# Gate and up projections of a feed-forward layer by seven half products, with weight sums on GpSimd

## The chip, the cores and the metric

The kernel runs on one core of a Trainium2 chip. The metric is the device time of one execution in microseconds. The engines are TensorE (PE for its matmuls, PEld for its weight loads), VectorE (DVE), ScalarE (ACT), GpSimd (POOL) and SyncE (SP, which issues the large loads). Each runs its instructions in a fixed order and waits on semaphores for the others.

## The reference

Two transformer blocks over 512 tokens of width 1024. The end of the second block is the part that changes:

```python
D_FF = -(-8 * D_MODEL // (3 * 256)) * 256          # 2816
...
def swiglu(h, w_gate, w_up, w_down):
    return (jax.nn.silu(h @ w_gate) * (h @ w_up)) @ w_down
...
h2 = modulate(rms_norm_2(x, g_pre_ffn[l]), sh_f, sc_f)
x = x + gt_f * rms_norm_2(swiglu(h2, w_gate[l], w_up[l], w_down[l]), g_post_ffn[l])
```

`h` is 512 x 1024, the gate and up weights are 1024 x 2816, the down weights 2816 x 1024, all float32.

## The kernel before

Every float32 operand of these products is split into a high part rounded to fp32r and the rest (`hi`, `lo`), and each product is three matmuls: hi·hi, hi·lo and lo·hi (`mm3`, lines 235 to 237). The normed tokens lie in SBUF with the 1024 input features on partitions, as eight slices `k` of 128, in two pairs of tiles `hi0`, `lo0` (slices 0 to 3) and `hi1`, `lo1` (slices 4 to 7), each 128 x 4 x 512. In the page and the trace all of these read `hi` and `lo`, and buffers' numbers are left out.

The weights come in chunks of 512 columns (`chunk`, line 210: one load of 2 MB into one of three buffers). For each slice k of a chunk, `split` makes `whi` on ScalarE (line 228, a copy that rounds) and `wlo` on VectorE (line 229, the chunk less `whi`, both in SBUF). There are three buffers of each, so that the splits can run up to three slices ahead of TensorE. TensorE then does 12 matmuls of 512 tokens for that slice (four groups of 128 columns, three matmuls each).

`phase3` ends with `mix_out`, `gate_first` and `ffn`. `gate_first` does the gate's first 512 columns in two halves of 256 tokens, since the last tokens' norms are still being made; in its second half each slice is split again, for 12 matmuls of 256 tokens. In `ffn` the order is up 0, gate 1, up 1, and so on to gate 5 and up 5 (the sixth chunk has 256 columns). After a gate chunk ScalarE applies silu from PSUM into `act` (line 1790), after an up chunk VectorE multiplies from PSUM (line 1792). Then comes the down projection.

The order on each engine comes from the scheduler of the tile framework; it puts instructions of a later step early where it can, but an engine that has reached an instruction waits for what that instruction needs, with all behind it.

Of the kernel before, what the change touches and what calls it, by code (L numbers as in the profile page):

```python
# [20 lines left out]
P = 128  # L21
# [94 lines left out]
class K:  # L116
# [101 lines left out]
    def split(self, src, gain=None, dst=None, eng=None):  # L218

        nc = self.nc  # L220
        m, n = src.shape
        if dst is None:
            dst = [self.sp.tile([P, 512], F32R, tag=f"w{b}", name=self.name(f"w{b}"))[:m, :n] for b in ("hi", "lo")]
        if gain is not None:
            self.split_to(*dst, src, gain)
            return dst
        hi, lo = dst
        nc.scalar.activation(hi, src, AF.Copy)  # L228
        (eng or nc.vector).tensor_tensor(lo, src, hi.bitcast(F32), ALU.subtract)  # L229
        return hi, lo  # L230
# [1080 lines left out]
    def phase3(self, u, banks):  # L1311
        tc = self.tc
        pool = lambda nm: tc.tile_pool(name=nm, bufs=1, reuse_waits="tile")
        with contextlib.ExitStack() as again:
            with pool("mix") as self.pm:

                self.mix = [None, None]
                heads = pool("heads")
                self.ph = heads.__enter__()
                with pool("p3f") as p:  # L1320
                    self.fourier(p, u)
                banks.close()
                with pool("p3b") as p:
                    self.attend2(p)
                heads.__exit__(None, None, None)
                again.enter_context(self.banks())
                with pool("p3c") as p:
                    y = p.tile([P, NT, D], F32, name="y_mix")
                    ready = self.mix_out(p, y)
                    halves = [self.half(0), self.half(1)]  # L1330
# [414 lines left out]
    def gate_first(self, hx, tiles, ready):  # L1745
# [16 lines left out]
                    self.mm3(ac[j][:, c], (wh[:, s], wl[:, s]), hx(k, c), k == 0, k == KD - 1)  # L1762
        return ac

    def ffn(self, p, hx, first):
# [4 lines left out]
        gm = self.post_gain(p, 1)  # L1770
        act = T([P, NF, S], "act")
        wg, wu = (I[n][0].rearrange("(k p) n -> p k n", p=P) for n in ("w_gate_2", "w_up_2"))
        for c in range(6):
            f = 4 if c < 5 else 2
            cs = slice(c * 512, c * 512 + f * P)
            for m, src in enumerate((wg, wu)):
                if c + m:
                    w = self.chunk(src[:, :, cs])
                    ac = self.others() if m else [self.accum() for _ in range(f)]
                    for k in range(KD):  # L1780
                        wh, wl = self.split(w[:, k, :])
                        for j in range(f):
# [4 lines left out]
                for j in range(f):  # L1787
                    a = act[:, 4 * c + j, :]
                    if m == 0:
                        sc.activation(a, ac[j], AF.Silu)  # L1790
                    else:
                        v.tensor_tensor(a, ac[j], a, ALU.mult)
        wd = I["w_down_2"][0].rearrange("(j p) n -> p j n", p=P)
        y = T([P, NT, D], "y")
        ss = self.sm.tile([P, NT, 2], F32, tag="ssy", name=self.name("ssy"))
        junk = lambda: T([P, S], "h", bufs=2)
        for n in range(2):
            cs = slice(n * 512, n * 512 + 512)
            ac = [self.accum() for _ in range(NT)]
            for c in range(3):  # L1800
                nj = 8 if c < 2 else 6
                w = self.chunk(wd[:, c * 8:c * 8 + nj, cs])
                last = n == 1 and c == 2
                if last:
                    wb = self.split_big(w)
                ab = []
                for i in range(nj):
                    j = 8 * c + i
                    if i % 4 == 0:
                        hb = self.half(j // 4 % 2)  # L1810
# [36 lines left out]
```

## Time and profile before

| | |
|---|---|
| three runs | 1512.69, 1518.17 and 1518.07 us (median 1518.07) |
| the profiled execution | 1516.21 us, its span 1514.4 us |
| mean granted TensorE clock | 0.971 |
| PE busy over the span | 1432.1 us, 95% |
| DVE, ACT, POOL busy | 720.6 us, 502.1 us, 123.8 us |
| second half of the gate's first chunk to the end of up 5 | about 1147 us to 1382.6 us of the span |
| down projection and tail | 1382.6 us to the end |

The page names a group of instructions by line, engine and operation with its tiles; the trace gives for each its start, its duration, and what the engine waited for before it. A row of the timeline with x3 is three instructions in a row, and its duration is that of all three.

### The profile page before, as it was taken

What the parts mean: (1) busy time and instruction counts of PE and PEld (TensorE: products, weight loads), DVE (VectorE), ACT (ScalarE), POOL (GpSimd) and SP (SyncE); (2) the same over time, 40 slices, a digit from 0 to 9 for tenths busy, and PEclk for the clock granted to TensorE, in tenths of its full rate; (3) what the DMA queues carried; (4) which work ended last, traced back from release to release, by engine and by line L of the source; (5) the groups of instructions that cost most, each with busy time, mean ns of one, the idle gap of its engine ahead of it and who ended that gap; (6) DMA issues with size and microseconds to landing.
All of it is one profiled execution on the core that took longest, in us unless ns stands there. A gap on an engine that the chain in (4) does not pass through costs nothing. (4 is left out here: it accounts for less than half of the span.)

```text
span 1514.4 us, 20068 instructions
## 1 busy us (share of the span) xinstructions
PE 1432.1 (95%) x7322; PEld 962.0 (64%) x7322; DVE 720.6 (48%) x1907; ACT 502.1 (33%) x1031; POOL 123.8 (8%) x145
## 2 busy tenths in 40 slices
PE   8999999998988999999999698999989999999997
PEld 6776657587434434433433387888878888888886
DVE  5465487867224322321222486667575333325356
ACT  5344454644101000100000454556445222224351
POOL 0012122301000000000000230110011000000000
PEclk9999997996999999999999899999999999999999
DMA  7647761061999999999999601110032331223211
GB/s 249 204 154 216 248 219 56 1 256 78 343 405 420 413 409 421 415 409 418 418 409 416 250 33 41 57 56 2 16 137 99 111 112 57 83 84 109 101 42 56
DMA packets 91957, 303.81 MB, mean 201 GB/s; under 512 B 6432, under 2 KB 12208, under 8 KB 79440
## 3 DMA queue, kind: packets, MB, share of 16 engines
q1 hardware_dynamic: 90016, 299.02, 51.4%
q0 software_dynamic: 1712, 3.35, 0.8%
q8 instruction: 59, 0.97, 0.3%
q14 instruction: 42, 0.34, 0.1%
q10 hardware_dynamic: 128, 0.13, 0.0%
HBM read 297.82 MB, written 2.56 MB: 198 GB/s over the span
## 5 line engine op out<-in xcount | busy, mean ns | idle before, releaser
L1268 PE MATMUL acc<-w,xg 128*32 128x512 f32 (+1 forms) x1024 | 216.1, 601 | 3.9 <-DMA w<-in_w_dram 3.9
L229 DVE TENSOR_TENSOR wlo<-w,whi 128x512 fp32r<-128x512 f32 (+3 forms) x161 | 104.0, 648 | 207.7 <-ACT whi L228 190.3
L228 ACT ACTIVATE whi<-w 128x512 fp32r<-128x512 f32 (+2 forms) x177 | 104.7, 596 | 219.0 <-PE o L236 86.2
L1268 PEld LDWEIGHTS acc<-w,xg 128*32 128x32 f32 (+1 forms) x1024 | 56.9, 124 | 122.8 <-issue 98.4
L1290 PE MATMUL acc<-w,hid 128*32 128x512 f32 (+1 forms) x512 | 120.8, 607 | 0.8 <-ACT hid L1281 0.7
L235 PE MATMUL acc<-whi,hi 128*128 128x512 f32 x280 | 112.4, 404 | 0.4 <-ACT hid L726 0.4
L236 PE MATMUL acc<-wlo,hi 128*128 128x512 f32 x280 | 112.3, 401 | 0.0
L237 PE MATMUL acc<-whi,lo 128*128 128x512 f32 x280 | 111.4, 398 | 0.0
L235 PE MATMUL acc<-hi,whi 128*128 128x512 f32 (+1 forms) x272 | 100.2, 372 | 2.8 <-ACT hi L1702 2.4
L237 PE MATMUL acc<-hi,wlo 128*128 128x512 f32 (+1 forms) x272 | 100.9, 372 | 0.6 <-POOL wlo L229 0.6
L236 PE MATMUL acc<-lo,whi 128*128 128x512 f32 (+1 forms) x272 | 101.0, 372 | 0.3 <-DVE lo L1703 0.2
L1275 DVE SCALAR_TENSOR_TENSOR hid<-acc,gc,hid 128x512 f32<-128x512 f32 x12 | 9.0, 751 | 158.1 <-PE acc L1268 142.6
L1290 PEld LDWEIGHTS acc<-w,hid 128*32 128x32 f32 (+1 forms) x512 | 37.8, 125 | 72.7 <-issue 59.3
L1305 DVE TENSOR_TENSOR x_sb<-ps,x_sb 128x512 f32<-128x512 f32 x96 | 60.6, 684 | 22.9 <-PE ps L1304 22.7
L235 PE MATMUL ps<-hi,whi 128*128 128x512 f32 x160 | 64.0, 400 | 0.0
L237 PE MATMUL ps<-hi,wlo 128*128 128x512 f32 x160 | 63.5, 397 | 0.0
L236 PE MATMUL ps<-lo,whi 128*128 128x512 f32 x160 | 63.5, 397 | 0.0
L235 PEld LDWEIGHTS acc<-whi,hi 128*128 128x128 f32 x280 | 52.9, 190 | 15.3 <-issue 1.4
L236 PEld LDWEIGHTS acc<-wlo,hi 128*128 128x128 f32 x280 | 53.0, 189 | 13.6 <-issue 1.8
L237 PEld LDWEIGHTS acc<-whi,lo 128*128 128x128 f32 x280 | 52.9, 189 | 12.9 <-issue 0.5
L235 PEld LDWEIGHTS acc<-hi,whi 128*128 128x128 f32 x272 | 51.0, 189 | 14.9 <-ACT hi L1702 3.0
L229 DVE TENSOR_TENSOR hid<-acc,hid 128x512 fp32r<-128x512 f32 x12 | 8.3, 691 | 106.8 <-PE acc L1290 95.7
(506 smaller groups left out, 2838.2 us busy)
## 6 DMA issues: line engine op xcount, KB each, us to landing
w<-in_w_dram SPq DMA_DIRECT2D x96, 1024.0 KB
w<-in_w_dram SPq DMA_DIRECT2D x192, 512.0 KB
w<-in_w_ada_dram SPq DMA_DIRECT2D x12, 2048.0 KB
w<-in_w_in_dram SPq DMA_DIRECT2D x5, 2048.0 KB
w<-in_w_gate_dram SPq DMA_DIRECT2D x5, 2048.0 KB
w<-in_w_up_dram SPq DMA_DIRECT2D x5, 2048.0 KB
w<-in_w_down_dram SPq DMA_DIRECT2D x4, 2048.0 KB
w<-in_w_o_dram SPq DMA_DIRECT2D x2, 2048.0 KB
```

The costliest lines, as they stand in the source:

```text
L228: nc.scalar.activation(hi, src, AF.Copy)
L229: (eng or nc.vector).tensor_tensor(lo, src, hi.bitcast(F32), ALU.subtract)
L235: mm(out, a[0], b[0], start=first, stop=False)
L236: mm(out, a[0], b[1], start=False, stop=False)
L237: mm(out, a[1], b[0], start=False, stop=last)
L1268: te.matmul(a[r, :], xg[:, k, c0 + r.start:c0 + r.stop], w[k // kp][e][:, k % kp, :], start=k == 0, stop=k == KD - 1)
L1275: v.scalar_tensor_tensor(h[:m], ac[1][:m], gate[:m], h[:m], ALU.mult, ALU.mult)
L1290: te.matmul(y[n][r, :], hT[:, k, r], w2[k // kp][e][:, k % kp, n * 512:n * 512 + 512], start=k == 0, stop=k == 3)
L1305: v.tensor_tensor(self.x[:, t, cs], ps, self.x[:, t, cs], ALU.add)
```

## The change

The first chunk of gate and of up stay as they are. For the other chunks, both operands are cut in halves: the weights by input features and by columns into four quarters, the tokens by input features and by position. The product is then made with the Winograd form of Strassen's scheme, seven products of halves in place of eight. `seven_tokens` makes four sums of token quarters (`t1` to `t4`) once, on GpSimd, splits them on ScalarE and VectorE, and keeps them in tiles `xg`, `xg`, `tk` and in the place of a quarter that is no longer needed. `seven_weights` makes the sums `s1`, `s2`, `s3` of a chunk's quarters on GpSimd; it is called in the middle of the chunk before (`between`, after the fourth product is issued). The fourth weight sum (line 1856) follows in the chunk itself. `seven` makes the products: each takes four slices of weights in two pieces of two slices (`split_pair`, lines 1871 and 1872, again 512 elements), and each piece feeds 12 matmuls of 256 tokens. VectorE adds the products from PSUM (lines 1847, 1857, 1860, 1861). In gate chunks ScalarE applies silu in SBUF; in up chunks GpSimd multiplies into `act` (line 1849). The load of the post-norm gain (line 1661) moves behind all of this on GpSimd's queue.

```diff
+    def seven_tokens(self, pe, act):
...
+        def split(src, t):
+            hi, lo = (t[:, 0], t[:, 1]) if t is not None else B[0][1]
+            nc.scalar.activation(hi, src, AF.Copy)
+            nc.vector.tensor_tensor(lo, src, hi.bitcast(F32), ALU.subtract)
+            return hi, lo
+
+        sub(u, B[0][1][1], B[0][0][1])
+        sub(t1, B[0][1][0], B[0][0][0])
+        add(t1, t1, u)
+        T1 = split(t1, tiles[0])
+        sub(t2, B[1][1][0], t1)
+        add(t2, t2, B[1][1][1])
+        T2 = split(t2, tiles[1])
+        sub(u, B[1][1][1], B[0][1][1])
+        sub(t3, B[1][1][0], B[0][1][0])
+        add(t3, t3, u)
+        sub(u, B[1][0][0], t2)
+        add(u, u, B[1][0][1])
+        T4 = split(u, tiles[3])
...
+    def seven_weights(self, pe, w):
...
+        gp.tensor_tensor(s1, q[0][1], q[1][1], ALU.add)
+        gp.tensor_tensor(s2, s1, q[0][0], ALU.subtract)
+        gp.tensor_tensor(q[0][1], q[0][0], q[0][1], ALU.subtract)
+        return q, s1, s2
...
+    def seven(self, pe, weights, tokens, a, m, between):
...
+        def product(src, tok):
+            out = self.accum()[:, :nj * 256].rearrange("p (j q) -> p j q", j=nj)
+            for i in range(2):
+                hi, lo = (b.rearrange("p (k n) -> p k n", k=2) for b in self.split_pair(src[:, 2 * i:2 * i + 2]))
+                for k in range(2):
+                    for j in range(nj):
...
+                        te.matmul(out[:, j], hi[:, k, s], b[0], start=kk + j == 0, stop=False)
+                        te.matmul(out[:, j], lo[:, k, s], b[0], start=False, stop=False)
+                        te.matmul(out[:, j], hi[:, k, s], b[1], start=False, stop=end)
...
+        def put(i, j, x, y):
+
+            o = a[:, rows[i], cols[j]]
+            t = small("sum", 2) if m else o
+            v.tensor_tensor(t, x, y, ALU.add)
+            if m:
+                gp.tensor_tensor(o, t, o, ALU.mult)
+            else:
+                sc.activation(o, o, AF.Silu)
...
+        sc.activation(p1, product(w11, tokens["11"]), AF.Copy)
+        put(0, 0, product(w12, tokens["21"]), p1)
+        gp.tensor_tensor(w12, w12, s2, ALU.subtract)
+        v.tensor_tensor(u6, product(s2, tokens["t2"]), p1, ALU.add)
+        p5 = product(s1, tokens["t1"])
+        between()
+        v.tensor_tensor(u7, product(s3, tokens["t3"]), u6, ALU.add)
+        v.tensor_tensor(u6, p5, u6, ALU.add)
+        put(1, 1, p5, u7)
+        put(1, 0, product(w22, tokens["t4"]), u7)
+        put(0, 1, product(w12, tokens["22"]), u6)
...
     def ffn(self, p, hx, first):
...
-        for c in range(6):
...
+        with pool("p3e") as pe:
             for m, src in enumerate((wg, wu)):
...
+                    tokens, third = self.seven_tokens(pe, act)
...
+            third()
+            blocks = [(c, m) for c in range(1, 6) for m in range(2)]
...
+            ahead()
+            while todo:
+                c, m, weights = todo.pop(0)
+                self.seven(pe, weights, tokens, act[:, 4 * c:4 * c + n(c), :], m, ahead)
```

The first place where the order matters is ScalarE's queue at the hand-over from the gate's first chunk (`w_9421`) to up 0 (`w_10015` before, `w_10035` now). Before:

```order
L228 ACTIVATE whi_9971<-w_9421 128x512
L228 ACTIVATE whi_9987<-w_9421 128x512
L228 ACTIVATE whi_10021<-w_10015 128x512
L228 ACTIVATE whi_10037<-w_10015 128x512
L1790 ACT_TABLE_LOAD
L1790 ACTIVATE act_10010<-acc_9695 128x512
L1790 ACTIVATE act_10010<-acc_9696 128x512
L1790 ACTIVATE act_10010<-acc_9697 128x512
L1790 ACTIVATE act_10010<-acc_9698 128x512
L228 ACTIVATE whi_10053<-w_10015 128x512
```

Now:

```order
L1783 ACTIVATE xg_10012<-act_10008 128x1024
L228 ACTIVATE whi_9971<-w_9421 128x512
L228 ACTIVATE whi_9987<-w_9421 128x512
L1783 ACTIVATE xg_10013<-act_10008 128x1024
L228 ACTIVATE whi_10041<-w_10035 128x512
L228 ACTIVATE whi_10057<-w_10035 128x512
L1899 ACT_TABLE_LOAD
L1899 ACTIVATE act_10008<-acc_9695 128x512
L1783 ACTIVATE tk<-act_10008 128x1024
L1899 ACTIVATE act_10008<-acc_9696 128x512
L1899 ACTIVATE act_10008<-acc_9697 128x512
L228 ACTIVATE whi_10073<-w_10035 128x512
```

Three splits of token sums (line 1783: t1, t2, t4) now stand between weight splits: the one of t4 (`tk`) stands ahead of the third slice of up 0 (`whi_10073`). One of the four silus, which all stand ahead of `whi_10073`, is not among the rows shown.

The second place is GpSimd's queue there. Before, only the gain's load followed the last weight split. Now (`act_10008` holds the token sums while they are made, `s_1998` and `s_1999` are gate 1's s1 and s2, `w_10175` its chunk):

```order
L229 TENSOR_TENSOR wlo_9860<-w_9421,whi_9859 128x512
L1777 TENSOR_TENSOR act_10008<-lo_1881_9418 128x1024
L1777 TENSOR_TENSOR act_10008<-hi_1880_9417 128x1024
L1777 TENSOR_TENSOR act_10008<-hi_1882_9419,hi_1880_9417 128x1024
L1776 TENSOR_TENSOR act_10008<-act_10008 128x1024
L1811 TENSOR_TENSOR s_1998_10177<-w_10175 128x1024
L1777 TENSOR_TENSOR act_10008<-hi_1882_9419,act_10008 128x1024
L1777 TENSOR_TENSOR act_10008<-lo_1883_9420,lo_1881_9418 128x1024
L1776 TENSOR_TENSOR act_10008<-act_10008,lo_1883_9420 128x1024
L1776 TENSOR_TENSOR act_10008<-act_10008 128x1024
L1812 TENSOR_TENSOR s_1999_10178<-s_1998_10177,w_10175 128x1024
L1777 TENSOR_TENSOR act_10008<-hi_1882_9419,act_10008 128x1024
```

Behind these stand s3 of gate 1 (line 1813) and the last addition of t4 (line 1776); t1 is complete with the fourth of the new instructions, t2 with the eighth, t4 with the thirteenth.

The third place is VectorE's queue in the middle of a full up chunk (`w_11346`, up 3; `s_2197` and `s_2196` are its s2 and s1):

```order
L1872 TENSOR_TENSOR wlo_11536<-s_2197_11349,whi_11535 128x512
L1872 TENSOR_TENSOR wlo_11552<-s_2197_11349,whi_11551 128x512
L1847 TENSOR_TENSOR sum_11530<-acc_11497,p_2213_11460 128x512
L1872 TENSOR_TENSOR wlo_11570<-s_2196_11348,whi_11569 128x512
L1872 TENSOR_TENSOR wlo_11586<-s_2196_11348,whi_11585 128x512
L1857 TENSOR_TENSOR u_2214_11461<-acc_11534,p_2213_11460 128x512
L1872 TENSOR_TENSOR wlo_11610<-w_11346,whi_11609 128x512
L1872 TENSOR_TENSOR wlo_11626<-w_11346,whi_11625 128x512
L1872 TENSOR_TENSOR wlo_11648<-w_11346,whi_11647 128x512
L1872 TENSOR_TENSOR wlo_11664<-w_11346,whi_11663 128x512
L1860 TENSOR_TENSOR u_2215_11462<-acc_11608,u_2214_11461 128x512
```

Where a chunk had eight weight splits in a row on VectorE, it now has fourteen with seven additions between them. Over the same stretch GpSimd has the fourth sum and the first multiplication of the chunk at hand, and then the next chunk's s1, s2 and s3.

## Rows read from the trace of the kernel before

**Rows 1.** The page, part 1: busy time, share of the span and instructions of each engine.

```profile
PE 1432.1 (95%) x7322; PEld 962.0 (64%) x7322; DVE 720.6 (48%) x1907; ACT 502.1 (33%) x1031; POOL 123.8 (8%) x145
```

**Rows 2.** Engines by stretch: up 0, and the chunks 1 to 5.

```profile
core 0: us, PE busy (x) PEld busy (x) DVE busy (x) ACT busy (x) POOL busy (x), PEclk, DMA share, GB/s
1158.00:1181.00 23.00, 23.00 (x104) 18.60 (x103) 7.57 (x12) 8.14 (x14) 0.00 (x0) 1.00 0.48 174
1181.00:1383.00 202.00, 202.00 (x867) 162.29 (x866) 64.35 (x103) 59.16 (x103) 0.00 (x0) 1.00 0.24 86
```

**Rows 3.** PE's timeline: end of the gate's first chunk, start of up 0, start of down.

```profile
1157.29 0.28 PE L236 MATMUL acc<-lo,whi 128*128 128x256 f32 x1
...
1158.46 0.28 PE L237 MATMUL acc<-hi,wlo 128*128 128x256 f32 x1
1158.57 0.39 PE L235 MATMUL ps<-hi,whi 128*128 128x512 f32 x1
...
1382.57 0.40 PE L235 MATMUL acc<-whi,hi 128*128 128x512 f32 x1
```

**Rows 4.** Groups of GpSimd by line and shape: count, busy us, mean ns of one.

```profile
L229 POOL TENSOR_TENSOR wlo<-w,whi 128x512 fp32r<-128x512 f32 x16 | 20.9, 1322 | 69.3 <-ACT whi L228 68.4 <-PE ps L1690 0.9
L777 POOL TENSOR_TENSOR w<-h,w 128x256 fp32r<-128x256 f32 x8 | 5.8, 734 | 12.4 <-ACT w L776 12.3
L600 POOL TENSOR_TENSOR hi<-hi,g 128x511 f32<-128x511 f32 x2 | 2.2, 1088 | 7.3 <-DVE g L598 3.9 <-PE o L544 3.4
L600 POOL TENSOR_TENSOR hi<-hi,g 128x127 f32<-128x127 f32 x2 | 0.8, 408 | 25.7 <-ACT hi L597 23.2 <-DVE g L598 2.5
```

**Rows 5.** GpSimd's timeline, 1131 to 1148 us: start us, us, instruction.

```profile
1138.39 3.78 POOL L229 TENSOR_TENSOR wlo<-w,whi 128x512 fp32r<-128x512 f32 x3 [2.34 <-ACT whi L228]
```

**Rows 6.** VectorE's timeline in the same stretch and just after.

```profile
1138.96 0.73 DVE L269 SCALAR_TENSOR_TENSOR r_y<-r_t,r_y 128x1 f32<-128x1 f32 x1
1140.03 0.91 DVE L269 SCALAR_TENSOR_TENSOR r_y<-r_t,r_y 128x1 f32<-128x1 f32 x1
1141.17 1.55 DVE L1703 TENSOR_TENSOR lo<-h,hi 128x512 fp32r<-128x512 f32 x1
...
1146.99 1.29 DVE L1703 TENSOR_TENSOR lo<-h,hi 128x512 fp32r<-128x512 f32 x2
```

**Rows 7.** GpSimd and VectorE, 850 to 870 us.

```profile
852.57 6.24 POOL L229 TENSOR_TENSOR w<-w,w 128x416 fp32r<-128x416 f32 x6 [402.38 <-DMA w<-in_w_in_dram]
868.57 1.75 POOL L1703 TENSOR_TENSOR lo<-h,hi 128x512 fp32r<-128x512 f32 x1 [6.22 <-ACT hi L1702]
...
852.73 4.88 DVE L1305 TENSOR_TENSOR x_sb<-ps,x_sb 128x512 f32<-128x512 f32 x8
868.49 0.69 DVE L229 TENSOR_TENSOR wlo<-w,whi 128x512 fp32r<-128x512 f32 x1
```

**Rows 8.** Groups of ScalarE by line and shape: weight splits, a pass over 1024 elements.

```profile
L228 ACT ACTIVATE whi<-w 128x512 fp32r<-128x512 f32 x151 | 94.4, 630 | 198.4 <-PE o L236 79.3 <-PE acc L236 71.5 <-PE acc L237 45.8
L1683 ACT ACTIVATE y_mix<-x_sb 128x1024 f32<-128x1024 f32 x4 | 4.3, 1066 | 4.8 <-DVE x_sb L1675 4.8
```

**Rows 9.** SP's timeline, 1100 to 1515 us: the load of gate 1.

```profile
1126.74 0.47 SPq L215 DMA_DIRECT2D w<-in_w_gate_dram  x1
```

**Rows 10.** Engines by stretch, as rows 2: waits of TensorE, and its granted clock.

```profile
1112.00:1114.00 2.00, 0.80 (x4) 0.34 (x2) 1.86 (x11) 0.64 (x3) 0.00 (x0) 1.00 0.02 4
1114.00:1116.00 2.00, 0.51 (x5) 0.54 (x6) 1.89 (x10) 0.00 (x0) 0.00 (x0) 1.00 0.00 0
1116.00:1118.00 2.00, 2.00 (x10) 1.71 (x8) 2.00 (x5) 1.85 (x5) 0.00 (x0) 0.52 0.00 0
1118.00:1120.00 2.00, 2.00 (x7) 1.62 (x6) 1.88 (x10) 1.73 (x4) 0.00 (x0) 0.63 0.00 0
...
352.00:356.00 4.00, 2.22 (x16) 2.08 (x15) 3.97 (x13) 2.19 (x4) 3.82 (x3) 0.86 0.00 0
356.00:360.00 4.00, 1.77 (x11) 1.72 (x9) 3.79 (x13) 2.83 (x3) 2.41 (x2) 0.50 0.00 0
```

More of the change, by code (lines that the diff above doesn't have):

```diff
@@ L1763, in gate_first, with quarter @@
         return ac
+    def seven_tokens(self, pe, act):
+        nc = self.nc
+        gp = nc.gpsimd
+        H = 256
+        def quarter(i, j):
+            return tuple(b[:, :, H * j:H * j + H] for b in self.hs[i])
+        B = [[quarter(i, j) for j in range(2)] for i in range(2)]
+        raw = [act[:, 14 + 2 * i:16 + 2 * i, :].rearrange("p a (b q) -> p (a b) q", q=H) for i in range(4)]
+        f = lambda a: a.bitcast(F32) if a.dtype == F32R else a
+        add = lambda d, a, b: gp.tensor_tensor(d, f(a), f(b), ALU.add)
+        sub = lambda d, a, b: gp.tensor_tensor(d, f(a), f(b), ALU.subtract)
+        tiles = [self.xg(F32R).rearrange("p (b k) (h q) -> p b (k h) q", b=2, h=2) for _ in range(2)]
+        tiles += [None, pe.tile([P, 2, 4, H], F32R, name="tk")]
+        t1, t2, t3, u = raw
+        def split(src, t):
[16 more added lines that the diff above has]
+        T4 = split(u, tiles[3])
+        tokens = {"11": B[0][0], "21": B[1][0], "22": B[1][1], "t1": T1, "t2": T2, "t4": T4}
+        return tokens, lambda: tokens.update(t3=split(t3, None))
@@ new lines, in seven_weights @@
+    def seven_weights(self, pe, w):
+        gp = self.nc.gpsimd
+        n = w.shape[2] // 2
+        q = [[w[:, 4 * i:4 * i + 4, n * j:n * j + n] for j in range(2)] for i in range(2)]
+        s1, s2 = (pe.tile([P, 4, 256], F32, tag=nm, name=self.name(nm))[:, :, :n] for nm in ("s1", "s2"))
+        gp.tensor_tensor(s1, q[0][1], q[1][1], ALU.add)
+        gp.tensor_tensor(s2, s1, q[0][0], ALU.subtract)
+        gp.tensor_tensor(q[0][1], q[0][0], q[0][1], ALU.subtract)
+        return q, s1, s2
@@ L1765, in ffn, with split_pair @@
+    def split_pair(self, src):
+        k, n = src.shape[1], src.shape[2]
+        hi, lo = (self.sp.tile([P, 512], F32R, tag=f"w{b}", name=self.name(f"w{b}"))[:, :k * n] for b in ("hi", "lo"))
+        r = lambda b: b.rearrange("p (k n) -> p k n", k=k)
+        self.nc.scalar.activation(r(hi), src, AF.Copy)
+        self.nc.vector.tensor_tensor(r(lo), src, r(hi).bitcast(F32), ALU.subtract)
+        return hi, lo
     def ffn(self, p, hx, first):
@@ L1786, in ffn @@
                     ac = first
-                for j in range(f):
-                    a = act[:, 4 * c + j, :]
+                    tokens, third = self.seven_tokens(pe, act)
+                for j in range(4):
+                    a = act[:, j, :]
                     if m == 0:
@@ L1792, in ffn, with ahead @@
                         v.tensor_tensor(a, ac[j], a, ALU.mult)
+            third()
+            blocks = [(c, m) for c in range(1, 6) for m in range(2)]
+            n = lambda c: 4 if c < 5 else 2
+            todo = []
+            def ahead():
+                if blocks:
+                    c, m = blocks.pop(0)
+                    w = self.chunk((wg, wu)[m][:, :, c * 512:c * 512 + n(c) * P])
+                    todo.append((c, m, self.seven_weights(pe, w)))
+            ahead()
+            while todo:
+                c, m, weights = todo.pop(0)
+                self.seven(pe, weights, tokens, act[:, 4 * c:4 * c + n(c), :], m, ahead)
+        late = pool("p3g")
+        p = late.__enter__()
+        gm = self.post_gain(p, 1)
         wd = I["w_down_2"][0].rearrange("(j p) n -> p j n", p=P)
```

29 lines of the change are left out of this document (21 added, 8 removed).

## The prediction

> **What bounds the kernel now.** I read the page's busy shares first, then the engines by stretch, then the timelines of the stretch that changes, then every place where GpSimd works beside VectorE. TensorE is busy for 1432.1 of 1514.4 us [rows 1]. In up 0 and in the chunks 1 to 5 it is busy for the whole stretch at granted clock 1.00, while VectorE and ScalarE work about a third of the time and GpSimd not at all [rows 2]. So the stretch lasts as long as its matmuls: from the start of up 0 at 1158.57 to the start of down at 1382.57 us are 224.0 us for 960 matmuls of 512 tokens (96 of up 0, 864 of the chunks 1 to 5), 0.2333 us each [rows 3]. Matmuls of 256 tokens start every 0.117 us, from 1157.29 to 1158.46 in ten steps [rows 3]: exactly half, so narrow matmuls cost nothing extra.
>
> **TensorE's part: 25.2 us less.** The chunks 1 to 5 of gate and up are 864 matmuls of 512 tokens, 864 x 0.2333 = 201.6 us. Seven products take 168 matmuls of 256 tokens per full chunk where there were 192: 7/8 of it, 176.4 us. A full chunk falls from 22.4 to 19.6 us, a half chunk to 9.8. Twelve matmuls of a piece take 1.40 us; every 1.40 us TensorE needs one new split pair, where in a chunk of the old kind it needed one per 2.80.
>
> **What GpSimd's sums cost.** All are over 1024 elements per partition; no row has one as long. Subtractions there take 0.73 us for 256 elements; the mean of 1.32 for 512 holds waits, and three in a row take 3.78, 1.26 each [rows 4, 5]. The line through 0.73 and 1.26 gives 2.32 at 1024. Float32 multiplications took 0.41 at 127 and 1.09 at 511 [rows 4], a line that gives 2.0. I take 2.34 for a sum, by the subtraction as the nearest operation, 2.0 as the low end, and 1.09 for the multiplications of up chunks. The Trainium skill's page "GPSIMD Engine Reference", section on performance versus the Vector engine, measures 4497 ns for an addition over 2048 elements; as an estimate that is 2.3 us at 1024, which also speaks for the upper line. By it the sum below stays at +44; by 2.0 it would be +28.
>
> **What they do to VectorE.** While GpSimd ran its three subtractions from 1138.39, two VectorE instructions of one element with two inputs in SBUF took 0.73 and 0.91 us and ended as GpSimd's first and second ended (1139.65, 1140.91), and a subtraction over 512 elements that had arrived at 1141.17 took 1.55 and ended 0.55 after GpSimd's third; two of the same kind with GpSimd idle took 1.29 together, 0.61 from start to start [rows 5, 6]. The other way round, a GpSimd subtraction that came 0.08 us after a VectorE one took 1.75 [rows 7]. But eight VectorE additions of a PSUM and an SBUF tile ran beside GpSimd at 0.61 each [rows 7]. So instructions with two SBUF inputs on VectorE and GpSimd's sums exclude each other, first come first served, and when both queues are full they alternate. Every `wlo` is such an instruction; the seven additions from PSUM are not. While GpSimd has work, VectorE makes one weight split per 2.34 + 0.61 = 2.95 us. TensorE wants one per 1.40, and waits 1.55 us for each sum, once the splits it has in hand are used up. That no row shows a sum of 1024 leaves open whether it excludes VectorE for its whole length. The Trainium skill's page "SBUF — State Buffer", "Who interferes with whom", says the port pair is held for the whole instruction; by that rule the sum is as below, and if it were let go halfway it would be some 15 us less (a rival).
>
> **The start: 25.6 us more.** GpSimd can begin its token sums when the last tokens' low parts are there, about 1147.7. ScalarE's queue now holds the split of t4 ahead of up 0's third slice, and t4 is GpSimd's thirteenth instruction from there, since gate 1's weight sums stand among them. Thirteen at 2.34 are 30.4 us. VectorE's two-input work in between is 6 weight splits of the gate, 2 of up 0 and two token splits of 1.15 (two of 512, less one start): 7.2 us. So t4 comes at 1185.3. Then ScalarE needs 1.07 for a pass over 1024 elements [rows 8], 1.5 for the remaining silus, 0.63 for the slice [rows 8], and VectorE 0.61: TensorE starts the third slice at 1189.8. Before, it started at 1158.57 + 2 x 2.80 = 1164.2. That is 25.6 us, all on the path, because ScalarE takes nothing out of order; TensorE waits some 5 us ahead of the gate's seventh slice (for t1), 7 ahead of up 0 (for t2) and 6 here. The loads are no part of it: gate 1's was issued at 1126.74 [rows 9].
>
> **The blocks: 43.6 us more.** I follow the queues through a full chunk. The fourth sum finds about half a split in hand and costs 0.7. The next chunk's s1 costs 1.0 to 1.4, s2 and s3 1.55 each. After that VectorE runs alone at 0.61 a piece and fills its three buffers again. That is 5.0 in the first chunk and 4.7 in a full up chunk; in a gate chunk after an up chunk three multiplications of 1.09 push the splits back and it is 5.5. Seven chunks with a full chunk behind them: 5.0 + 3 x 4.7 + 3 x 5.5 = 35.6. The eighth makes the sums of a half chunk, which are short: 1.5. The two half chunks, with sums of 1.26 against pieces of 0.70: 4.8 and 1.7. ScalarE stays below its limit (14 splits of 0.63 and at most five other passes of 0.6 in 24 us) [rows 8], and the additions from PSUM fit beside GpSimd. The weight loads keep two chunks of lead; the gain's load, now behind all sums, is needed 60 us later. Both cost nothing.
>
> **The clock: 2 us more.** After 2.7 us of idling within 1112 to 1116 TensorE was granted 0.52 and 0.63 of its clock over the next 4 us, that is mostly 1.2 in place of 2.4 GHz [rows 10]. In the start only the last of three such falls is not hidden by a later wait; by those rows, 4 x (1 - 0.575), it costs 1.7.
>
> **The sum.** -25.2 + 25.6 + 43.6 + 2 = +46.0 us on the profiled execution's 1516.2: **1562 us**. That execution lies 1.9 us below the median of 1518.07, less than the runs' spread of 5.5; I do not correct for it. About 0.5%, 7.6 us, is what a measurement of this kernel can tell from no change. The case's own range is 1546 (sums at 2.0) to 1578 (below).
>
> **The rivals.**
> Shorter turns: GpSimd lets VectorE in halfway through a sum. Then a split comes every 1.17 + 0.61 = 1.78 us, a wait of 0.38 in place of 1.55, and the full chunks come to about 22.3 us. Start and half chunks as above: 1547, and with sums at 2.0 1532. For it: no row with 1024 elements. Against it: at 512 nothing was let in.
> Falling clock: in the run of s1, s2, s3 TensorE works 1.40 of every 2.95 us for some 9 us. From 352 to 360 it was busy for 2.22 and 1.77 of 4 us, and the clock went to 0.86 and 0.50 [rows 10]. A piece at half clock, 2.80, still fits in 2.95, so only what follows the run pays, 1.7 at most in eight chunks: +14, 1576.
> The other side, no exclusion: the two-input subtractions of VectorE go on beside these sums, as those from PSUM did [rows 7]. Then the blocks take their 176.4 us, and only the queue order at the start is left: thirteen sums of 2.34 end at 1178.2, and the third slice starts 18 us late (13.6 with sums at 2.0). -25.2 + 18 + 1 + 2 gives 1512, with the shorter sums 1508. With the start at 18 the change stops being slower by 0.5% when the blocks lose less than 12.8 of the 43.6 us. Against it stand all of rows 5 and 6.
> Full saving: the start is hidden too, 1491. It needs thirteen sums in 16.5 us, 1.27 each, half of either line; the queues above make that unlikely. That the change might not remove the matmuls is excluded by its order: 168 per full chunk are there.
>
> **How the numbers follow.** The forecast 0.59, shorter turns 0.17, falling clock 0.10, no exclusion 0.10 (half of it under 0.5% faster, half over), full saving 0.04. Slower by over 0.5%: 0.59 + 0.17 + 0.10 = 0.86; faster 0.05 + 0.04 = 0.09; same 0.05. The range from 1530 to 1580 takes in the first three, whose tails beyond it and the last two leave out about 0.2.
>
> **What would show it.** `wlo` (line 1872) at a mean over 1 us with some at 2.5 to 3, and idle time of TensorE of some 70 us in the stretch, put down to VectorE's `wlo` and, at the start, to ScalarE's split of up 0. Up 0's third slice starting near 1190. Chunks of 24 to 25 us. GpSimd's sums at 2.3 us or, with waits, near 2.9. It is wrong if `wlo` stays at 0.69 beside busy GpSimd, or if chunks take under 21 us.

## The result and the profile after

The changed kernel takes **1554.72 us** (median of four runs, 1553.96 to 1559.55), the kernel before 1517.8 in the same comparison: a ratio of 1.0258, 95% interval 1.0228 to 1.0288. It is slower by 2.6%. The profiled execution of the changed kernel took 1559.55 us, with a span of 1557.7.

Part 1 of the page of the changed kernel:

```profile
PE 1431.7 (92%) x7970; PEld 989.2 (64%) x7970; DVE 879.5 (56%) x2023; ACT 545.1 (35%) x1107; POOL 276.8 (18%) x215
```

Beside [rows 1], TensorE's busy time is the same although it has less to multiply, and VectorE is busy for 159 us more although it has only 116 instructions more. GpSimd's busy time is up by 153 us. The engines by stretch (columns as in [rows 2]): the start, up 0's rest, and the chunks 1 to 5:

```profile
1147.00:1190.00 43.00, 26.60 (x147) 22.64 (x147) 32.53 (x20) 13.38 (x22) 36.21 (x13) 0.84 0.14 49
1190.00:1206.00 16.00, 14.74 (x56) 11.58 (x57) 6.38 (x9) 5.73 (x10) 0.00 (x0) 0.89 0.13 39
1206.00:1430.00 224.00, 197.90 (x1547) 187.92 (x1547) 202.77 (x220) 102.37 (x181) 117.36 (x58) 1.00 0.25 87
```

Where TensorE had no gap before [rows 2], it now stands still for 26 of 224 us in the chunks, and VectorE is busy for 203 of them. In the start GpSimd is busy for 36 of 43 us. What TensorE waits for most from 1147 to 1430 (us in total, times, longest), by the view of waits:

```profile
PE acc L1836 <- DVE wlo L1872: 25.2, 33, 1.1
PE acc L237 <- DVE wlo L229: 8.3, 5, 4.4
PE ps L235 <- ACT whi L228: 4.7, 2, 3.2
PE ps L237 <- DVE wlo L229: 3.8, 1, 3.8
```

These waits are for the low part `wlo` of a weight split on VectorE, but for 4.7 us in which ScalarE had not made up 0's `whi`. The groups of VectorE and GpSimd by line and shape, 1206 to 1380 us (count, busy us, mean ns of one):

```profile
L1872 DVE TENSOR_TENSOR wlo<-w,whi 128x512 fp32r<-128x512 f32 x72 | 98.3, 1394 | 7.1 <-ACT whi L1871 4.9 <-PE ps L236 2.1
L1872 DVE TENSOR_TENSOR wlo<-s,whi 128x512 fp32r<-128x512 f32 x28 | 31.0, 1117 | 9.4 <-ACT whi L1871 9.4
L1813 POOL TENSOR_TENSOR w<-w 128x1024 f32<-128x1024 f32 x7 | 19.8, 2826 | 0.0
L1812 POOL TENSOR_TENSOR s<-s,w 128x1024 f32<-128x1024 f32 x7 | 19.0, 2715 | 0.5
L1811 POOL TENSOR_TENSOR s<-w 128x1024 f32<-128x1024 f32 x7 | 16.8, 2402 | 15.1 <-DVE wlo L1872 15.1
```

A `wlo` of 0.69 us when nothing disturbs it [rows 7] lasts 1.12 and 1.39 on average. The timelines of the changed kernel show how: two runs of GpSimd and VectorE in one chunk, then ScalarE and TensorE at the start.

```profile
1242.96 2.40 POOL L1811 TENSOR_TENSOR s<-w 128x1024 f32<-128x1024 f32 x1 [0.63 <-DVE wlo L1872]
1245.44 2.71 POOL L1812 TENSOR_TENSOR s<-s,w 128x1024 f32<-128x1024 f32 x1
1248.12 2.82 POOL L1813 TENSOR_TENSOR w<-w 128x1024 f32<-128x1024 f32 x1
...
1243.41 8.68 DVE L1872 TENSOR_TENSOR wlo<-w,whi 128x512 fp32r<-128x512 f32 x4
...
1163.04 1.06 ACT L1783 ACTIVATE xg<-act 128x1024 fp32r<-128x1024 f32 x1 [5.79 <-POOL act L1776]
1174.67 1.06 ACT L1783 ACTIVATE xg<-act 128x1024 fp32r<-128x1024 f32 x1 [9.53 <-POOL act L1776]
1188.18 1.06 ACT L1783 ACTIVATE tk<-act 128x1024 fp32r<-128x1024 f32 x1 [9.50 <-POOL act L1776]
...
1191.26 0.52 PE L235 MATMUL ps<-hi,whi 128*128 128x512 f32 x1 [3.25 <-ACT whi L228]
1209.79 0.28 PE L1835 MATMUL acc<-hi,whi 128*128 128x256 f32 x1
```

Four `wlo` with nothing between them take 8.68 us while three sums run: the first waits for s1, the second for s2, the third for s3, and only the fourth goes at its own pace. At the start ScalarE stands three times for GpSimd's token sums (5.8, 9.5 and 9.5 us): the first time with splits of the gate's first chunk queued behind, then with up 0's, and up 0's third slice starts at 1191.26.

**Where the time went.** The part of the program ahead of the change was 4.1 us late in this run (the last tokens' transpositions ahead of up 0 start at 1147.74 in place of 1143.63); in the profiled runs shown here this lead lies between 2.7 us early and 4.1 us late, it is there before the first changed instruction, and it has no part in the change. From there to chunk 1 (1209.79 in place of 1180.97) the change costs **24.7 us**. From chunk 1's first matmul to the end of the span it takes 347.91 us in place of 333.43: **14.5** more. 4.1 + 24.7 + 14.5 = 43.3, the difference of the spans. A full chunk takes 24.0 or 24.55 us, in turn, where it took 22.4.

### The profile page after: what moved, and what is told of

Its sections match the earlier page's. It is cut to its first block, busy times and chain, and to the rows that moved or that the text cites. A ratio compares the mean times of both kernels' runs of the same rounds, so it can differ in the third digit from the quotient of the medians.

```text
span 1557.7 us, 21705 instructions
## 1 busy us (share of the span) xinstructions
PE 1431.7 (92%) x7970; PEld 989.2 (64%) x7970; DVE 879.5 (56%) x2023; ACT 545.1 (35%) x1107; POOL 276.8 (18%) x215
## 4 chain that ended last, share of the span: by engine, by line
PE 57%; DVE 17%; DMA 16%; ACT 4%; issue 3%; POOL 3%; SPq 0%; DVEq 0%; ACTq 0%; POOLq 0%
DMA w<-in_w_dram 16%; PE acc L236 7%; PE acc L235 7%; PE acc L237 7%; DVE wlo L1872 6%; PE acc L1268 6%; PE acc L1290 3%; PE acc L1836 2%; PE o L544 2%; PE acc L1837 2%; PE acc L1835 2%; PE ps L1006 2%; PE o L1607 2%; PE t L1594 1%; PE acc L724 1%
## 5 line engine op out<-in xcount | busy, mean ns | idle before, releaser
L1872 DVE TENSOR_TENSOR wlo<-w,whi 128x512 fp32r<-128x512 f32 (+1 forms) x100 | 121.1, 1239 | 11.4 <-ACT whi L1871 9.2
L229 DVE TENSOR_TENSOR wlo<-w,whi 128x512 fp32r<-128x512 f32 (+2 forms) x81 | 70.1, 877 | 55.7 <-ACT whi L228 55.7
L1836 PE MATMUL acc<-hi,wlo 128*128 128x256 f32 x288 | 82.5, 287 | 14.0 <-DVE wlo L1872 13.9
L1871 ACT ACTIVATE whi<-w 128x512 fp32r<-128x512 f32 (+1 forms) x100 | 58.7, 587 | 90.1 <-PE acc L1837 80.4
L228 ACT ACTIVATE whi<-w 128x512 fp32r<-128x512 f32 (+2 forms) x97 | 57.2, 601 | 71.7 <-PE acc L237 51.2
L1837 PE MATMUL acc<-lo,whi 128*128 128x256 f32 x288 | 80.7, 280 | 0.0
L1835 PE MATMUL acc<-hi,whi 128*128 128x256 f32 x288 | 80.4, 280 | 0.0
L229 POOL TENSOR_TENSOR w<-w,w 128x416 fp32r<-128x416 f32 x8 | 8.3, 1073 | 399.5 <-DMA w<-in_w_in_dram 399.5
L1836 PEld LDWEIGHTS acc<-hi,wlo 128*128 128x128 f32 x288 | 54.2, 188 | 18.2 <-DVE wlo L1872 18.0
```

Source lines behind the costliest of these rows:

```text
L1835: te.matmul(out[:, j], hi[:, k, s], b[0], start=kk + j == 0, stop=False)
L1836: te.matmul(out[:, j], lo[:, k, s], b[0], start=False, stop=False)
L1837: te.matmul(out[:, j], hi[:, k, s], b[1], start=False, stop=end)
L1871: self.nc.scalar.activation(r(hi), src, AF.Copy)
L1872: self.nc.vector.tensor_tensor(r(lo), src, r(hi).bitcast(F32), ALU.subtract)
```

## The experiments

Theory A is that of the prediction: sums on GpSimd and subtractions of two SBUF tiles on VectorE exclude each other, and at the start ScalarE's queue waits for token sums. Rival B: VectorE simply has too much work. Rival C: ScalarE or PSUM is late. Rival D: the start is late for gate 1's weight sums. "Start" is chunk 1's first matmul against the kernel before, the run's own lead ahead of the change taken off as above; "rest" is from there to the end of the span, 333.4 before and 347.9 after. Chunks are measured from one chunk's copy of p1 (its first product) on ScalarE to the next one's. Where one time is given, it is one execution; the kernel before lay between 1512.69 and 1523.2 us over all comparisons, so starts, rests and chunks are compared rather than totals.

### No weight sums

```diff
-        gp.tensor_tensor(s1, q[0][1], q[1][1], ALU.add)
-        gp.tensor_tensor(s2, s1, q[0][0], ALU.subtract)
-        gp.tensor_tensor(q[0][1], q[0][0], q[0][1], ALU.subtract)
-        return q, s1, s2
+        return q, q[0][1], q[1][1]
...
-        gp.tensor_tensor(w12, w12, s2, ALU.subtract)
```

> Leaves out the four sums of weight quarters of each chunk (products 2, 3, 5, 7 take raw quarters, so the output is another); matmuls, splits, additions and the token sums stay. Theory A (GpSimd's sums and VectorE's subtractions of two SBUF tiles exclude each other): full chunks fall from 24.0 and 24.5 us to 19.6 to 20, the time of their matmuls; the start costs some 16 us over the kernel before where it cost 24.7, since the gate's weight sums no longer stand ahead of t4; the span is about 45 us under the changed kernel's, near 1510. Rival B (VectorE has too much work in a chunk, 14 splits and 7 additions, GpSimd or not): chunks stay at 24. Rival C (PSUM or ScalarE late): chunks stay at 24 too, with TensorE waiting for whi or for an accumulator.

Measured: 1513.67 us, span 1511.8; start +18.1 (2 more than expected), rest 314.7, every full chunk 19.92 to 19.95. B and C are out: the same splits and additions, with the same engines, keep up with TensorE once the sums are gone. (A rival that no theory above names, that the splits only wait for the sums as their input, would pass this test too; the run with PSUM copies leaves the sums in place and settles it.) What is left of the start, 18 us, is the token sums'. The engines by stretch, one chunk:

```profile
1222.00:1242.00 20.00, 20.00 (x171) 20.00 (x170) 16.33 (x21) 9.39 (x16) 6.60 (x4) 1.00 0.30 105
```

TensorE is busy throughout, so 19.95 us is what 168 matmuls of 256 tokens take: 0.1187 each, and not the 0.1167 that I had taken from [rows 3]. More on this in the last section.

### No token sums

```diff
-        sub(u, B[0][1][1], B[0][0][1])
...
-        T4 = split(u, tiles[3])
-        tokens = {"11": B[0][0], "21": B[1][0], "22": B[1][1], "t1": T1, "t2": T2, "t4": T4}
-        return tokens, lambda: tokens.update(t3=split(t3, None))
+        tokens = {"11": B[0][0], "21": B[1][0], "22": B[1][1], "t1": B[0][1], "t2": B[1][1], "t3": B[0][0], "t4": B[1][0]}
+        return tokens, lambda: None
```

> Leaves out the token sums and their splits (the products take raw token quarters, so the output is another); the weight sums stay. Theory A: the start falls from +24.7 to about +4 us over the kernel before, chunks stay at 24.0 and 24.5 us; the span is some 20 us under the changed kernel's, near 1537. Rival D (the start is late for the weight sums of gate 1 and their loads, not for t1, t2 and t4): the start stays at +20 or more.

Measured: 1535.48 us, span 1533.6; start +4.3, rest 347.2, full chunks 23.9 and 24.5. The span is 3 us under the expected one, which is what this run's lead was shorter (1.2 us for 4.1). D is out: gate 1's weight sums alone cost the start 4.3 us. The two runs together split the loss: the token sums own 18 to 20 us of the start and nothing of the chunks, the weight sums all of the chunks' waits.

### The high part from PSUM

```diff
         self.nc.scalar.activation(r(hi), src, AF.Copy)
-        self.nc.vector.tensor_tensor(r(lo), src, r(hi).bitcast(F32), ALU.subtract)
+        h = r(hi).bitcast(F32)
+        if copy:
+            h = r(self.psum()[:, :k * n])
+            self.nc.scalar.activation(h, r(hi).bitcast(F32), AF.Copy)
+        self.nc.vector.tensor_tensor(r(lo), src, h, ALU.subtract)
```

with `copy` set for the products of s2, s3 and w22.

> Nothing is left out. For the products that run beside GpSimd's sums (s2, s3, w22) ScalarE copies the high part once more, into a PSUM bank, and VectorE's wlo subtraction reads it from there; GpSimd's and VectorE's work keep their sizes, ScalarE gets six passes of about 0.6 us more per chunk. Theory A (the exclusion holds only between instructions whose inputs all lie in SBUF): full chunks fall from 24.0 and 24.5 to 20 to 21 us, the span some 29 us under the changed kernel's, near 1528, and the wlo of these products last about 0.6 us beside busy GpSimd. Rival B (too much work on VectorE): chunks stay at 24. Rival C (ScalarE or PSUM late): chunks get longer than 24.6.

Measured: 1527.93 us, span 1526.1; start +24.9, rest 323.0, chunks 20.2 (from a gate's p1 to the up's) and 21.8 (from an up's p1 to the gate's, where the multiplications on GpSimd fall). The span is 2 us under the expected one, the chunks of 21.8 are above the expected 20 to 21, with the same work as in the changed kernel and six passes of ScalarE more per chunk. Its groups from 1206 to 1380 us, and its timelines of GpSimd and VectorE:

```profile
L1876 DVE TENSOR_TENSOR wlo<-w,ps 128x512 fp32r<-128x512 f32 x32 | 22.0, 688 | 22.0 <-ACT ps L1875 12.3 <-PE acc L1836 7.1 <-issue 2.6
L1813 POOL TENSOR_TENSOR w<-w 128x1024 f32<-128x1024 f32 x7 | 16.9, 2418 | 0.0
```

```profile
1234.96 2.42 POOL L1812 TENSOR_TENSOR s<-s,w 128x1024 f32<-128x1024 f32 x1
1237.34 2.42 POOL L1813 TENSOR_TENSOR w<-w 128x1024 f32<-128x1024 f32 x1
...
1236.29 0.69 DVE L1876 TENSOR_TENSOR wlo<-w,ps 128x512 fp32r<-128x512 f32 x1 [0.76 <-ACT ps L1875]
1237.71 0.69 DVE L1876 TENSOR_TENSOR wlo<-w,ps 128x512 fp32r<-128x512 f32 x1 [0.73 <-ACT ps L1875]
1238.91 1.40 DVE L1876 TENSOR_TENSOR wlo<-w,whi 128x512 fp32r<-128x512 f32 x1
```

The subtraction with one input in PSUM runs in 0.69 us in the middle of a sum, and the sums, 2.72 and 2.83 before, are back at 2.42: neither engine hinders the other. The next one, with both inputs in SBUF again, arrives in the third sum at 1238.91 and ends at 1240.31, 0.55 us after that sum (1.40 in all). The sums that feed these splits stand where they stood, so the wait was not for their results. The Trainium skill's page "SBUF — State Buffer", section "Who interferes with whom", says that a VectorE instruction with at most one SBUF input does not contend with GpSimd; this trace agrees (688 ns beside busy GpSimd, where the changed kernel's splits with both inputs in SBUF took 1394).

### The copy made, but not read

```diff
-            h = r(self.psum()[:, :k * n])
-            self.nc.scalar.activation(h, r(hi).bitcast(F32), AF.Copy)
+            self.nc.scalar.activation(r(self.psum()[:, :k * n]), r(hi).bitcast(F32), AF.Copy)
```

> As the run with PSUM copies, and ScalarE makes the same six copies per chunk, but VectorE's wlo reads the high part from SBUF again; nothing is left out. If what helped there was that one input of wlo lay in PSUM, full chunks go back to 24.0 and 24.5 us and the span to near 1557. If what helped was another order or timing that came with the copies, chunks stay near 20.6 and 21.4 and the span near 1526.

Measured: 1552.68 us, span 1550.5; start +24.9, rest 347.3, chunks 23.99 and 24.54. All of the gain is gone, so it was the place of the operand, and no timing that came with the copies.

### The sums on VectorE

```diff
-        gp = self.nc.gpsimd
+        gp = self.nc.vector
...
-        gp.tensor_tensor(w12, w12, s2, ALU.subtract)
+        v.tensor_tensor(w12, w12, s2, ALU.subtract)
```

> The four sums of weight quarters run on VectorE in place of GpSimd, in the same order and places; nothing is left out. A sum of 1024 then takes VectorE about 1.15 us (two of 512) and none excludes another engine. Theory A: full chunks fall to about 22, the start to +18, and the span is some 23 us under the changed kernel's, near 1534: the burst of three sums still holds up the splits, but for 3.5 us and not 9. Rival B (too much work on VectorE): chunks get longer than 24.5, since VectorE gets 4.6 us more per chunk.

Measured: 1540.29 us, span 1538.5; start +23.5, rest 336.0, chunks in turn 22.1, 22.1, 23.7, 23.7. With 4.6 us more work per chunk VectorE is faster than it was beside GpSimd, which settles B once more; a sum takes it 1.22 us. Two misses. The start got only 1.2 us better instead of 7, since the token sums on GpSimd now hold up the weight sums as well. And the chunks of 23.7 are 1.6 us longer than the others: TensorE's clock fell in them. The engines behind the three sums of one chunk of 22.1 and of one of 23.6 (columns as in [rows 2]):

```profile
1236.00:1240.00 4.00, 2.38 (x18) 2.15 (x18) 3.19 (x5) 0.95 (x2) 0.00 (x0) 1.00 0.00 0
1240.00:1244.00 4.00, 4.00 (x36) 4.00 (x35) 3.66 (x6) 1.76 (x4) 0.27 (x1) 1.00 0.00 0
...
1280.00:1284.00 4.00, 2.37 (x18) 1.97 (x17) 4.00 (x6) 1.26 (x2) 0.00 (x0) 1.00 0.00 0
1284.00:1288.00 4.00, 4.00 (x22) 4.00 (x22) 1.73 (x3) 0.63 (x1) 0.00 (x0) 0.57 0.00 0
```

4 us at a granted clock of 0.57, mostly 1.2 in place of 2.4 GHz, cost 4 x 0.43 = 1.7 us; the other two long chunks have 0.57 and 0.58 over 4 us, the short ones 1.00. TensorE had been busy for the same 2.4 of 4 us before; why the clock fell in one and not in the other stays open.

### Sums of half the length

```diff
-        gp.tensor_tensor(s1, q[0][1], q[1][1], ALU.add)
+        for h in (slice(0, 2), slice(2, 4)):
+            gp.tensor_tensor(s1[:, h], q[0][1][:, h], q[1][1][:, h], ALU.add)
...
```

> Each sum of weight quarters (1024 elements, 2.40 us) is made by two GpSimd instructions of 512 elements; nothing is left out. If VectorE's wlo is kept out for the length of one instruction and the two alternate, a wlo comes every 1.3 + 0.4 to 0.6 = 1.7 to 1.9 us beside the sums in place of 2.75, and full chunks fall from 24.0 and 24.5 us to between 20.5 and 22.5; the start stays near +24 for its token sums of 1024. The span falls by 14 to 28 us, to 1530 to 1544. Were GpSimd's total work what counts (4 x 2.4 us a chunk, however cut), chunks would stay at 24. Were VectorE let in halfway through a sum already, cutting would change nothing either.

Measured: 1530.13 us, span 1528.3; start +20.3, rest 329.7, chunks 22.0 and 22.2; the start, expected near +24, gained 4 us as well. The timelines:

```profile
1231.72 3.43 POOL L1814 TENSOR_TENSOR s<-s,w 128x512 f32<-128x512 f32 x2
1235.12 3.44 POOL L1816 TENSOR_TENSOR w<-w 128x512 f32<-128x512 f32 x2
...
1229.21 6.50 DVE L1876 TENSOR_TENSOR wlo<-w,whi 128x512 fp32r<-128x512 f32 x4
```

GpSimd starts a half sum every 1.70 us (two from 1231.72 to 1235.12), and VectorE's four `wlo` take 6.50 us where they took 8.68: one instruction of each in turn. The same number of elements, cut finer, costs TensorE 18 us less in the chunks. So at both lengths a turn is one whole instruction: the rival of shorter turns falls.

### The tokens late

```diff
-                wh, wl = self.split(w[:, k, :], eng=None if i else self.nc.gpsimd)
+                wh, wl = self.split(w[:, k, :], eng=None if i and k < 6 else self.nc.gpsimd)
...
-            for m, src in enumerate((wg, wu)):
+            for c, m in ((0, 0), (0, 1), (1, 0)):
...
+                        if c and k == 3:
+                            tokens, self.third = self.seven_tokens(pe, act)
```

and the splits of t1 to t4 kept in the written order on their engines.

> Only the start is changed: gate 1 is made in the old way, by eight products (2.8 us more matmuls), so that the token sums are needed a chunk later; their splits stand in ScalarE's and VectorE's queues behind gate 1's fourth slice; GpSimd makes the last two low parts of the gate and only then the token sums, while up 0 and gate 1 need a split per 2.80 us. Nothing is left out. Theory A: from the last tokens on to gate 1 as in the kernel before, within 2 us (it was +24.7); gate 1 in 22.4 to 23.5; full chunks of seven products at 24.0 and 24.5 as before. The span falls some 24 us, to about 1531. Rival (the start is late for GpSimd's load beside VectorE as such): up 0 and gate 1 lose over 8 us, and the span stays above 1538.

Measured: 1533.83 us, span 1532.0. Up 0 starts 3.7 us late, up 0 and gate 1 take 45.6 us in place of 44.8, then chunks of 24.0 and 24.55. So of the start's 24.7 us 4.5 are left, over twice the 2 that theory A allowed; but beside GpSimd's load up 0 and gate 1 lose 0.8 us, and not the 8 of the rival. Where the other 3.7 come from is seen in the next run, which has the same start (up 0 3.7 us late).

### Late tokens, PSUM copies, multiplications on VectorE

```diff
             if m:
-                gp.tensor_tensor(o, t, o, ALU.mult)
+                v.tensor_tensor(o, t, o, ALU.mult)
```

on top of the late tokens and of the PSUM copies.

> The late tokens of the run before, the PSUM copies of whi for the products of s2, s3 and w22, and the multiplications of up chunks on VectorE in place of GpSimd (2.4 us more for it per up chunk). Nothing is left out. Theory A: start within 2 us of the kernel before, gate 1 at 22.4 to 23.5, full chunks of seven products at 20 to 20.6 us, gate and up alike; about 1503 to 1508 us, that is 0.7 to 1.0% under the kernel before. Rival B (too much work on VectorE): up chunks get longer than the gate's by 1 us or more, and the time stays above 1512.

Measured: 1514.92 us (12 runs, 1511.76 to 1520.22), ratio to before 0.9979, interval 0.9964 to 0.9995: 7 us above the upper end of what was expected. Gate chunks take 20.25, but up chunks 21.75. The timelines of the start and of the end of an up chunk:

```profile
1147.77 2.36 POOL L1777 TENSOR_TENSOR act<-hi 128x1024 f32<-128x1024 f32 x1 [4.78 <-PE acc L237]
1150.08 2.83 POOL L1777 TENSOR_TENSOR act<-hi,hi 128x1024 f32<-128x1024 f32 x1
...
1147.81 5.64 DVE L1703 TENSOR_TENSOR lo<-h,hi 128x512 fp32r<-128x512 f32 x2
...
1269.23 0.68 DVE L1864 TENSOR_TENSOR u<-acc,u 128x512 f32<-128x512 f32 x1
1269.83 1.27 DVE L1848 TENSOR_TENSOR sum<-acc,u 128x512 f32<-128x512 f32 x2
1271.03 1.28 DVE L1850 TENSOR_TENSOR act<-sum,act 128x512 f32<-128x512 f32 x2
1272.23 1.88 DVE L1879 TENSOR_TENSOR wlo<-w,whi 128x512 fp32r<-128x512 f32 x3
...
1272.96 0.39 PE L1837 MATMUL acc<-hi,wlo 128*128 128x256 f32 x1 [1.50 <-DVE wlo L1879]
```

Two token sums that need only high parts stood first on GpSimd and held the last tokens' low parts (1.3 us for two [rows 6]) for 5.64 us. TensorE waited 2.25 us for them, and its granted clock then was 0.50 from 1152 to 1154. And VectorE's queue had three additions and two multiplications ahead of the next `wlo`: 3 us in a row, more than the reserve. The time above 1512 and up chunks longer than the gate's by 1.5 us are what B had forecast; that it is the order and not the amount of work on VectorE is shown by the next two runs, which leave it the same work and bring up chunks down to 21.0 and 20.5.

### The order mended

```diff
-        add = lambda d, a, b: gp.tensor_tensor(d, f(a), f(b), ALU.add)
+        add = lambda d, a, b: keep(gp.tensor_tensor(d, f(a), f(b), ALU.add))
...
-                v.tensor_tensor(o, t, o, ALU.mult)
+                self.later.append((o, t))
...
+            while self.later and src is not w22:
+                o, t = self.later.pop(0)
+                self.tc.keep_in_program_order(v.tensor_tensor(o, t, o, ALU.mult))
```

> As the run that joins late tokens, PSUM copies and multiplications on VectorE, with two changes of order and nothing left out: all token sums stand on GpSimd behind the gate's last low parts (two of them stood ahead and kept the last tokens' low parts waiting: TensorE stood still for 3 us at 1147.7), and VectorE takes the multiplications of products 6 and 4 behind the last piece's wlo (they stood ahead, and TensorE waited 1.5 to 1.9 us in each up chunk). If these two waits are what is left, the start falls from +3.7 to under +1 us, up chunks from 21.7 to 20.3, together some 9 us: 1504 to 1507, 0.7 to 1.0% under the kernel before. If the wait only moves to the additions or to the next chunk's sums, up chunks stay over 21 and the time stays above 1510.

Measured: 1510.69 us (six runs, 1508.73 to 1511.79), ratio 0.9954, interval 0.9937 to 0.9971. The first wait is gone: up 0 starts where it did before (1158.58 with the lead taken off). The second went by half: up chunks take 21.0, not 20.3. The time is 3.7 us above the upper end of what was expected, for a new one came: up 0 and gate 1 now take 49.3 us in place of 44.8.

```profile
1157.68 28.16 DVE L229 TENSOR_TENSOR wlo<-w,whi 128x512 fp32r<-128x512 f32 x10 [3.51 <-ACT whi L228]
1185.76 1.87 DVE L1912 TENSOR_TENSOR act<-ps,act 128x512 f32<-128x512 f32 x3
...
1191.04 0.50 PE L237 MATMUL acc<-hi,wlo 128*128 128x512 f32 x1 [2.10 <-DVE wlo L229]
```

Ten `wlo` in 28.16 us, one per 2.82, is the alternation with the token sums again; TensorE wants one per 2.80, and the four multiplications of up 0 then find no reserve left. Behind this wait of 2.10 us the granted clock was 0.62 and 0.53 from 1192 to 1196, which makes 1.7 of the 4.5 us.

### Copies in up 0 too

```diff
+        h = hi.bitcast(F32)
+        if copy:
+            h = self.accum()[:m, :n]
+            nc.scalar.activation(h, hi.bitcast(F32), AF.Copy)
+        (eng or nc.vector).tensor_tensor(lo, src, h, ALU.subtract)
...
-                        wh, wl = self.split(w[:, k, :])
+                        wh, wl = self.split(w[:, k, :], copy=m == 1 and k > 2)
...
-            while self.later and src is not w22:
+            if self.later and src is not w22:
```

> As the run with two changes of order, and nothing left out; from up 0's fourth slice on ScalarE copies whi into an accumulator's PSUM bank that is free there, and wlo reads it from the bank; and VectorE takes at most one multiplication of an up chunk behind each product. In the run before, up 0's wlo came every 2.82 us beside the token sums where TensorE wants one every 2.80, the reserve was used up, and behind the four multiplications of up 0 TensorE lost 4.5 us by the end of gate 1. Theory A: with up 0's wlo out of the exclusion that loss falls below 1 us, and up chunks from 21.0 to about 20.4, together 4 to 6 us: 1504.5 to 1507, 0.7 to 0.9% under the kernel before. If the loss came from the four multiplications alone, it stays at 3 us or more and the time above 1508.

Measured: **1506.45 us** (six runs, 1504.28 to 1508.11), ratio to the kernel before 0.9918, interval 0.9895 to 0.9941: a version that beats both, the kernel before by 0.8%. Up 0 and gate 1 take 46.9 us (2.1 lost, not under 1), up chunks 20.5. Up 0 has copies from its fourth slice on. The groups of 1158 to 1182 us (up 0, and gate 1's first splits), without and with the copy:

```profile
L233 DVE TENSOR_TENSOR wlo<-w,whi 128x512 fp32r<-128x512 f32 x5 | 10.5, 2121 | 6.8 <-ACT whi L228 5.0 <-PE ps L240 1.9
L233 DVE TENSOR_TENSOR wlo<-w,acc 128x512 fp32r<-128x512 f32 x5 | 3.4, 684 | 6.7 <-ACT acc L232 6.7
```

The same instruction beside sums of the same length: 2121 ns on average with two SBUF inputs, 684 with one.

## Why the prediction was right

The forecast was 1562 us, the median is 1554.7, inside the range, and slower by 2.6%, by the mechanism it named. By its own steps:

- **TensorE's part, -25.2.** The 168 matmuls per chunk are there, but each takes 0.1187 us and not 0.1167, as the run without weight sums shows. 201.6 us become 179.4 and not 176.4: -22.2.
- **GpSimd's sums at 2.34.** Undisturbed 2.40 to 2.42, so the upper line of [rows 4, 5] was the right one.
- **What they do to VectorE.** Shown: the PSUM copies take the wait away, the unread copies bring it back. The period was off. I added the two times, 2.34 + 0.61 = 2.95; the sums that meet a waiting `wlo` last 2.71 and 2.82 with VectorE's turn in them, so `wlo` comes every 2.7 to 2.8 us and TensorE waits 1.3 to 1.4 per sum at full alternation, not 1.55. The Trainium skill's page "SBUF — State Buffer", section "SBUF: two separate sides", has whichever starts first, a GpSimd instruction or a VectorE one with two SBUF inputs, hold the shared pair of ports for the whole instruction; the traces agree, with a turn of 1.70 us for half sums where whole sums take 2.7 to 2.8.
- **The start, +25.6.** Up 0's third slice came at 1191.26 - 4.11 = 1187.15 for 1189.8: 23.0 us late, not 25.6. The shorter turns give 1.3 of the difference: GpSimd's thirteen instructions, with VectorE's turns between them, took from 1151.93 to 1188.15, 36.2 us for 30.4 + 7.2. An error of addition gives 0.7: the terms behind t4, added to 1185.3, make 1189.1. And the last 0.7 is that the slice's first matmul needs `whi` alone, so it started 3.1 us after t4 and not 3.8.
- **The clock, +2.** From that slice to chunk 1 it takes 1209.79 - 1191.26 = 18.5 us for six slices of 2.80, so 1.7 more: right. The granted clock was 0.50 from 1192 to 1194 and 0.74 to 1196. (23.0 and 1.7 make the 24.7.)
- **The blocks, +43.6.** The term that was mis-sized most. With the matmuls at -22.2 the rest's +14.5 leaves **36.7** us of waits. Full chunks of 24.0 and 24.55 hold 4.05 and 4.6 us of wait, where I had 4.7 and 5.5; the seven full chunks with a full one behind come to 29.5 for 35.6. That gate chunks behind an up chunk lose more was right.
- **Sum.** 24.7 + 36.7 - 22.2 = +39.2, on 1516.2 that is 1555.4; I had 46.0. The start and the clock came out 2.9 us smaller and the saving 3.0 us smaller, and that these two cancel is luck. The ends of the range, 1546 and 1578, were counted from the median 1518 and the forecast from 1516.2, a slip of 2 us that decides nothing. The 1559.55 of the profiled execution has 4.1 us more from the part ahead of the change.
- **The rivals.** Shorter turns: refuted by the half sums. Falling clock: here the granted clock stayed at 1.00 through the chunks; with the sums on VectorE it fell to 0.57 in some of them, so this rival can come true in a near kernel. No exclusion: refuted by the `wlo` of 1.39 us and the two runs with PSUM copies. Full saving: refuted by the 24.7 us of the start. I had looked for some 70 us of idle time of TensorE; the windows above show 43.8. The rest of the 61.4 us lost (24.7 and 36.7) lies in matmul records: one of 256 tokens is drawn 0.28 us long though the next starts after 0.12, so that a wait that costs 1.38 us shows 1.12, and time at the lower clock counts as busy. Busy time is no measure of the loss.

## What to carry over

Work on an idle engine is free only if it does not shut out an engine that the path needs: before giving GpSimd sums, count VectorE's instructions with two SBUF inputs in the same stretch and price each at a whole GpSimd instruction. If they must overlap, put one VectorE operand in PSUM (here one ScalarE pass of 0.60 us in place of a wait of 1.3), or cut GpSimd's instructions short. And give sums that feed an in-order queue a chunk of lead, even at the price of computing one chunk the old way: those 2.45 us (22.4 for 19.95) bought 20.

## What was not expected of the hardware

- When VectorE and GpSimd take turns, VectorE's 0.61 us does not add in full: sums of 2.40 come every 2.7 to 2.8 us, half sums of 1.3 every 1.70.
- Matmuls of 256 tokens do not all start at the same pace. In the run without weight sums, on TensorE's timeline, at granted clock 1.00 and with no wait:

```profile
1228.45 0.28 PE L1831 MATMUL acc<-hi,whi 128*128 128x256 f32 x1
...
1231.17 0.28 PE L1833 MATMUL acc<-lo,whi 128*128 128x256 f32 x1
1231.29 0.28 PE L1831 MATMUL acc<-tk,whi 128*128 128x256 f32 x1
...
1234.04 0.28 PE L1833 MATMUL acc<-tk,whi 128*128 128x256 f32 x1
```

23 steps of the product on t3, which lies in a quarter of the normalized tokens' tiles and so reads `hi` and `lo`, take 2.72 us, 0.118 each; 23 on t4 in `tk` take 2.75, 0.120. The other products on `hi` and `lo` show 0.118 on average too. Those on `xg` show 0.120. Three of seven products use `xg` or `tk`; with 72 matmuls at 0.120 and 96 at 0.118 a chunk takes 19.95 us and not 19.6. Why is open: the tiles differ in how their columns lie, but no run here changed that alone.
- GpSimd's multiplication of 512 elements, which the prediction put at 1.09 us, took 1.69 on average in the changed kernel. In the run with PSUM copies it took 1.30 where it came first, with the `wlo` that arrived behind it lasting 1.41, and 1.67 to 1.74 where it had to wait for a `wlo` with two SBUF inputs: it takes part in the exclusion like the sums.
